# The first half of the retention output projection as seven block products, with block sums made by accumulating DMAs

## The chip, the cores and the metric

The kernel runs on one core of a Trainium2 chip. The metric is the device time of one execution in microseconds; the median of three runs of the kernel before is 2591.95 us. The engines are TensorE (PE, with its weight loads shown as PEld), VectorE (DVE), ScalarE (ACT), GpSimd (POOL) and SyncE (SP), which here only issues DMAs. The weights and activations come from and go to HBM; SBUF holds the tiles and PSUM the sums of TensorE.

## The reference

A trunk of two layers over 1024 tokens and 1024 features, in float32. Layer 0 mixes tokens with forgetting attention, layer 1 with retention, each followed by a SwiGLU FFN. What matters here is the end of retention: `y` is normalized per head, multiplied by a gate, and projected from 2048 features back to 1024.

```python
def retention(h, w_in, w_out):
    ...
    y = y.transpose(1, 0, 3, 2, 4).reshape(B, S, H, dv)
    mu = jnp.mean(y, axis=-1, keepdims=True)
    var = jnp.mean(jnp.square(y - mu), axis=-1, keepdims=True)
    y = ((y - mu) * lax.rsqrt(var + EPS)).reshape(B, S, H * dv).astype(h.dtype)
    return (jax.nn.silu(g) * y) @ w_out
...
            x = x + retention(h, ret_w_in[j], ret_w_out[j])
        h = rmsnorm(x, norm_ffn[i])
        x = x + swiglu(h, ffn_w_in[i], ffn_w_out[i])
```

## The kernel before, in words

All activations are kept transposed: a tile is 128 features by 1024 tokens, used in two halves of 512 tokens (`HALF`). A float32 product is made of three fast ones: each operand is split into a high part (a rounded copy, ScalarE) and a low part (operand minus high part, VectorE) by `split`, lines 98 and 99, and TensorE adds high x high, high x low and low x high (`mm_u`, lines 106 to 108).

Most projections of the kernel do not multiply block by block but by seven products (`Products`, lines 635 to 637): two output tiles by two token halves form a 2 x 2 block, and so do the weights (A11 to A22) and the operand (B11 to B22). The sums S1 to S4 of weight blocks are made by `Blocks`; the sums T1 to T4 of operand blocks by `Combos`, from tiles in SBUF, or by `Stored`, which keeps seven arrays in HBM and loads and splits each when a product first asks for it (`get`, line 560). A product is four triples, 12 matmuls of 512 columns. `open` makes the first product, `middle` the next four, `close` the last two; each pair of output tiles holds three PSUM banks a, b, c from `open` to its last sums. Seven banks go round for these (`mm_ps`).

The retention core has eight stages, four heads by two token halves. `prepare(h)` loads keys, queries and values of a head; `scores`, `weighted` and `crossed` are its matmuls. `finish(h, ib)` takes a stage's four result tiles of 512 tokens, normalizes them (`colsum` and `rows` are small matmuls, lines 159 and 165; the scaling is line 1138), for head 0 multiplies them by the gate that it loads from `gd`, and stores them to `zd` (line 1143). Heads 0 and 1 make z tiles 0 to 7, heads 2 and 3 tiles 8 to 15.

The output projection then runs in two halves over the 16 z tiles. In the first, the eight tiles are loaded by `load_units` (lines 783 and 786), which multiplies head 1's by their gates (line 787) and splits them into 32 buffers of the pool `bpa`; for each of the eight output tiles the weights are loaded and split (`wtile2`, line 773), and `mm_u` makes 8 x 3 matmuls for each half of the tokens; the old residual `xo` is added (lines 1176 and 1177). The second half is `out_proj`, which does the same for tiles 8 to 15 (six of them in the pool `bpb`, of 24 buffers, two in `bpa`), and prepares the next FFN's operand.

What sets the order: the instructions of an engine run in the order of its queue. That order is made at build time by a planner that goes by the written order as priority and by its own estimates of when operands and buffers are free. Buffers limit it: five staging buffers of 1024 columns (`st`), six split buffers for weights (`wh`, `wl`), 16 tiles `y` (`yu`), two buffers `xo`. SP issues nearly all DMAs, from one queue; GpSimd has nothing to do in this part.

Of the kernel before, what the change touches and what calls it, by code (L numbers as in the profile page):

```python
# [17 lines left out]
P = 128  # L18
# [19 lines left out]
def trunk(ctx, tc, nc, d, out):  # L38
# [16 lines left out]
    def nm(s):  # L55
        cnt[0] += 1
        return f"{s}_{cnt[0]}"
# [21 lines left out]
    def wh_wl(width=512):  # L79
        return [wp.tile([P, 512 + 64], F32R, tag=t, name=nm(t))[:, :width] for t in ("wh", "wl")]  # L80
# [20 lines left out]
    def mm_u(ps, wts, acts, h, cols=slice(0, H), first=True, last=True):  # L101
        n = len(wts)
        for k in range(n):
            wh, wl = wts[k]
            xh, xl = (t[:, cols] for t in acts[k][h])
            nc.tensor.matmul(ps, wh, xh, start=(first and k == 0), stop=False)  # L106
            nc.tensor.matmul(ps, wh, xl, start=False, stop=False)  # L107
            nc.tensor.matmul(ps, wl, xh, start=False, stop=(last and k == n - 1))  # L108
# [429 lines left out]
    class Stored:  # L538


        def __init__(self, name, pools):
            self.pools = pools
            self.d = {n: dp.tile([P, 4 * H], F32, tag=name + n, name=name + n) for n in NAMES}
            self.t = {}

        def put(self, j, e, o):
            t1, t2, t4 = qu("t1"), qu("t2"), qu("t4")
            nc.vector.tensor_tensor(t1, e[1], e[0], op=ALU.subtract)
            nc.vector.tensor_tensor(t2, o[1], t1, op=ALU.subtract)
            nc.vector.tensor_tensor(e[1], o[1], e[1], op=ALU.subtract)  # L550
            nc.vector.tensor_tensor(t4, o[0], t2, op=ALU.subtract)
            for n, t in zip(NAMES, (e[0], t2, t1, e[1], o[0], o[1], t4)):
                nc.sync.dma_start(self.d[n][:, j * H:(j + 1) * H], t)

        def get(self, n):
            if n not in self.t:
# [7 lines left out]
    def wsplit(src):  # L564
        hi, lo = wh_wl()
        split(hi, lo, src)
        return hi, lo

    class Blocks:


        def __init__(self, src):
            self.s1, self.ready = None, {}
            sts = []
            for i in range(2):
                st = sp.tile([P, 1024], F32, tag="st", name=nm("st"), bufs=5)
                nc.sync.dma_start(st, src[:, i * 1024:(i + 1) * 1024])
                sts.append(st)
            self.a11, self.a12 = sts[0][:, 0:512], sts[0][:, 512:1024]
            self.a21, self.a22 = sts[1][:, 0:512], sts[1][:, 512:1024]  # L580

        def sums(self, early=False):
            if early:
                self.s1, self.s2 = qu("s1"), qu("s2")
            else:
                self.s1 = sp.tile([P, 512], F32, tag="sc", name=nm("s1"), bufs=4)
                self.s2 = sp.tile([P, 512], F32, tag="sc", name=nm("s2"), bufs=4)
            nc.vector.tensor_tensor(self.s1, self.a21, self.a22, op=ALU.add)  # L588
            nc.vector.tensor_tensor(self.s2, self.s1, self.a11, op=ALU.subtract)

        def early(self):
            self.ready["A11"] = wsplit(self.a11)
# [3 lines left out]
        def get(self, n):  # L596
            if n in self.ready:
                return self.ready[n]
            if n == "A11":
                return wsplit(self.a11)  # L600
            if n == "S2":
                return wsplit(self.s2)
            if n == "S1":
                return wsplit(self.s1)
            if n == "S3":
                nc.vector.tensor_tensor(self.a21, self.a11, self.a21, op=ALU.subtract)
                return wsplit(self.a21)
            if n == "A12":
                return wsplit(self.a12)
# [3 lines left out]
            return wsplit(self.a22)  # L613

    OPERANDS = {"A11": "B11", "S1": "T1", "S2": "T2", "A12": "B21", "S3": "T3", "A22": "T4", "S4": "B22"}

    class Products:
# [26 lines left out]

        def middle(self, u2, u3):

            self.run("S1", self.c, first=True)
            self.run("S2", self.b)
            u2(self.b)
            self.run("A12", self.a)  # L650
            self.run("S3", self.b)
            u3(self.b, self.c)
# [115 lines left out]
    def wtile2(src, nk):  # L768
        parts = []
        for k in range(0, nk, 4):  # L770
            n = min(4, nk - k)
            st = sp.tile([P, 1024], F32, tag="st", name=nm("st"), bufs=5)
            nc.sync.dma_start(st[:, :n * P], src[:, k * P:(k + n) * P])
            hi, lo = wh_wl(n * P)
            split(hi, lo, st[:, :n * P])
            parts += [(hi[:, j * P:(j + 1) * P], lo[:, j * P:(j + 1) * P]) for j in range(n)]
        return parts

    def load_units(pool, src, gate=None):

        r = []
        st = sp.tile([P, 1024], F32, tag="st", name=nm("st"), bufs=5)
        nc.sync.dma_start(st, src)
        if gate is not None:
            gt = sp.tile([P, 1024], F32, tag="st", name=nm("st"), bufs=5)
            nc.sync.dma_start(gt, gate)
            nc.vector.tensor_tensor(st, st, gt, op=ALU.mult)
        for h in range(2):
            r.append(bsplit(pool, st[:, HALF[h]]))
        return r  # L790
# [324 lines left out]
    def finish(h, ib, yps):  # L1115
        acc = sp.tile([P, H], F32, tag="sacc", name=nm("yacc"), bufs=2)
        ys = []
        for vt in range(4):
            y = yu("yt")
            nc.scalar.copy(y, yps[vt])  # L1120
            if vt == 0:
                nc.scalar.activation(acc, y, AF.Square)
            else:
                sq = yu("sq")
                nc.scalar.activation(sq, y, AF.Square)
                nc.vector.tensor_tensor(acc, acc, sq, op=ALU.add)
            ys.append(y)
        cs = colsum(acc, mp, "ms")
        var = small([P, 4], "yv")
        rs = slice(4 * ib, 4 * ib + 4)  # L1130
        nc.vector.scalar_tensor_tensor(var, cs[:, 0:4], 1.0 / 512, rho2[:, h, rs], op0=ALU.mult, op1=ALU.mult)
        nc.vector.tensor_scalar(var, var, EPS, None, op0=ALU.add)
        r = rsqrt(var, 4)
        fac = small([P, 4], "yf")
        nc.vector.tensor_tensor(fac, r, rho[:, h, rs], op=ALU.mult)
        fb = rows(fac, mp, "ms")
        for vt in range(4):
            nc.vector.tensor_tensor(ys[vt], ys[vt], fb, op=ALU.mult)
# [4 lines left out]
            nc.sync.dma_start(zd[4 * h + vt][:, HALF[ib]], ys[vt])  # L1143

    prepare(0)
    heads[0][4] = state(heads[0][1], heads[0][3])
    stages = [(h, ib) for h in range(RET_HEADS) for ib in range(2)]
# [15 lines left out]
        if ib == 1 and nxt:  # L1163
            heads[h + 1][4] = state(heads[h + 1][1], heads[h + 1][3])

    zg = list(zip(zd, [None] * (4 * 1) + gd[4 * 1:]))
# [12 lines left out]
    ffn(1, X, nrm, xd, None, True, nw, MAP3)  # L1179

# [93 lines left out]
```

## Time and profile before

| what | value |
|---|---|
| median of three runs | 2591.95 us (2591.46 to 2592.87) |
| profiled execution | 2590.04 us, of which the span is 2588.2 us |
| TensorE busy | 2561.4 us, 99% of the span |
| VectorE busy | 1839.9 us, 71% |
| ScalarE busy | 1229.7 us, 48% |
| GpSimd busy | 168.0 us, 6% |
| chain of waits, TensorE's share | 94% |

The profile is one execution on the chip. Times in its rows are from the start of the span. A group of instructions is shown with its line, engine, output and inputs, count, busy time and mean duration of one, and then the idle time of the engine just before it and what ended that. Matmuls overlap in their pipeline, so the sum of their durations is more than the time that they take; their cost is read from the distance of their starts. The granted TensorE clock was 0.999 of full speed.

### The profile page before, as it was taken

The numbers are of one execution on the slowest core, as the hardware profiler recorded it, in microseconds if no ns is written. First come the engines' busy times: TensorE is split into PE (matmuls) and PEld (weight loads), VectorE is DVE, ScalarE is ACT, GpSimd is POOL, SyncE is SP. The second block draws the span as 40 slices with busy tenths as digits, with TensorE's granted clock in tenths as the row PEclk, the third lists the DMA queues.
The fourth block names the chain that finished last, engine by engine and source line by source line (L and its number), as shares of the span: only waits on it lengthen the run. The fifth ranks groups of instructions, "written<-read, shape, count | busy, mean of one in ns | idle before, by whom it ended". The sixth has DMA issues, their size and how long they took to land.

```text
span 2588.2 us, 35137 instructions
## 1 busy us (share of the span) xinstructions
PE 2561.4 (99%) x12808; PEld 2182.1 (84%) x12808; DVE 1839.9 (71%) x3131; ACT 1229.7 (48%) x2320; POOL 168.0 (6%) x147
## 2 busy tenths in 40 slices
PE   9999999999999999999999999999999999999998
PEld 8888887888888888889898989898888888888788
DVE  6798888966666768886656576785567666667795
ACT  6566656643333455454343435662354333335543
POOL 0143323000000000001000010000000000000000
PEclk9999999999999999999999999999999999999999
DMA  3111142423332345533332335555522333325441
GB/s 130 45 58 58 58 143 87 160 100 102 110 106 97 120 150 187 165 112 116 101 119 98 110 100 167 191 184 193 202 96 86 106 102 106 105 82 187 167 151 66
DMA packets 137695, 312.12 MB, mean 121 GB/s; under 512 B 15665, under 2 KB 28721, under 8 KB 137521
## 3 DMA queue, kind: packets, MB, share of 16 engines
q1 hardware_dynamic: 136800, 309.33, 35.6%
q8 instruction: 100, 1.64, 0.3%
q14 instruction: 75, 0.61, 0.1%
q10 hardware_dynamic: 720, 0.55, 0.1%
HBM read 217.54 MB, written 92.27 MB: 120 GB/s over the span
## 4 chain that ended last, share of the span: by engine, by line
PE 94%; DVE 2%; issue 1%; ACT 1%; DMA 1%; POOL 0%; SPq 0%; DVEq 0%; POOLq 0%; ACTq 0%
PE mm L635 18%; PE mm L636 18%; PE mm L637 18%; PE mm L107 7%; PE mm L106 7%; PE mm L108 7%; PE mm L751 2%; PE mm L749 2%; PE mm L750 2%; PE mm L256 1%; PE mm L257 1%; PE mm L258 1%; PE mm L1101 1%; PE mm L1102 1%; PE mm L1100 1%
## 5 line engine op out<-in xcount | busy, mean ns | idle before, releaser
L635 PE MATMUL mm<-b,wh 128*128 128x512 f32 x2128 | 826.2, 390 | 3.8 <-ACT 22_4491_22622 L683 2.2
L636 PE MATMUL mm<-b,wh 128*128 128x512 f32 x2128 | 828.3, 389 | 0.0
L637 PE MATMUL mm<-b,wl 128*128 128x512 f32 x2128 | 824.9, 389 | 0.0
L98 ACT CAST wh<-st 128x512 fp32r<-128x512 f32 (+1 forms) x449 | 276.2, 616 | 519.4 <-PE mm L636 315.8
L635 PEld LDWEIGHTS mm<-b,wh 128*128 128x128 f32 x2128 | 399.6, 188 | 86.7 <-ACT 22_4491_22622 L683 2.6
L637 PEld LDWEIGHTS mm<-b,wl 128*128 128x128 f32 x2128 | 399.5, 188 | 82.8
L636 PEld LDWEIGHTS mm<-b,wh 128*128 128x128 f32 x2128 | 399.6, 188 | 82.1
L99 DVE TENSOR_TENSOR wl<-st,wh 128x512 fp32r<-128x512 f32 (+1 forms) x449 | 318.0, 712 | 188.9 <-ACT wh L98 186.1
L98 ACT CAST wh<-s 128x512 fp32r<-128x512 f32 x252 | 156.4, 622 | 307.2 <-PE mm L636 271.5
L106 PE MATMUL mm<-b,wh 128*128 128x512 f32 x736 | 287.0, 393 | 8.4 <-ACT b L126 6.1
L107 PE MATMUL mm<-b,wh 128*128 128x512 f32 x736 | 287.8, 392 | 1.6 <-DVE b L99 1.6
L108 PE MATMUL mm<-b,wl 128*128 128x512 f32 x736 | 287.7, 392 | 0.0
L99 DVE TENSOR_TENSOR wl<-s,wh 128x512 fp32r<-128x512 f32 x252 | 180.0, 716 | 92.9 <-ACT wh L98 88.8
L106 PEld LDWEIGHTS mm<-b,wh 128*128 128x128 f32 x736 | 138.9, 189 | 38.3 <-ACT b L126 6.6
L107 PEld LDWEIGHTS mm<-b,wh 128*128 128x128 f32 x736 | 138.8, 189 | 29.8 <-DVE b L99 2.1
L108 PEld LDWEIGHTS mm<-b,wl 128*128 128x128 f32 x736 | 138.8, 189 | 28.5
L98 ACT CAST b<-st 128x512 fp32r<-128x512 f32 x216 | 124.7, 611 | 79.3 <-DMA st<-ac_T 24.5
L99 DVE TENSOR_TENSOR b<-st,b 128x512 fp32r<-128x512 f32 x216 | 140.7, 675 | 30.3 <-ACT b L98 28.3
L750 PE MATMUL mm<-wl,b 128*128 128x256 f32 x448 | 126.6, 283 | 0.0
L749 PE MATMUL mm<-wh,b 128*128 128x256 f32 x448 | 126.2, 283 | 0.0
L751 PE MATMUL mm<-wh,b 128*128 128x256 f32 x448 | 126.2, 283 | 0.0
L588 DVE TENSOR_TENSOR s<-st 128x512 f32<-128x512 f32 x84 | 58.1, 692 | 66.4 <-DMA st<-ffn_in 27.2
(496 smaller groups left out, 3889.0 us busy)
## 6 DMA issues: line engine op xcount, KB each, us to landing
st<-ffn_in SPq DMA_DIRECT2D x88, 512.0 KB, 3.5
st<-ffn_out_pairs SPq DMA_DIRECT2D x32, 512.0 KB, 3.9
st<-ac_T SPq DMA_DIRECT2D x32, 512.0 KB, 4.9
ac_T<-t SPq DMA_DIRECT2D x48, 256.0 KB, 2.4
st<-ac_B SPq DMA_DIRECT2D x24, 512.0 KB, 4.0
st<-fox_qk SPq DMA_DIRECT2D x32, 256.0 KB, 2.7
xo<-xd SPq DMA_DIRECT2D x32, 256.0 KB, 3.0
ac_B<-t SPq DMA_DIRECT2D x32, 256.0 KB, 2.4
```

Source lines behind the costliest of these rows:

```text
L98: nc.scalar.copy(hi, src)
L99: return nc.vector.tensor_tensor(lo, src, hi.bitcast(F32), op=ALU.subtract)
L106: nc.tensor.matmul(ps, wh, xh, start=(first and k == 0), stop=False)
L107: nc.tensor.matmul(ps, wh, xl, start=False, stop=False)
L108: nc.tensor.matmul(ps, wl, xh, start=False, stop=(last and k == n - 1))
L588: nc.vector.tensor_tensor(self.s1, self.a21, self.a22, op=ALU.add)
L635: nc.tensor.matmul(ps, hi[:, js], th, start=first and j == 0, stop=False, skip_group_check=True)
L636: nc.tensor.matmul(ps, hi[:, js], tl, start=False, stop=False, skip_group_check=True)
L637: nc.tensor.matmul(ps, lo[:, js], th, start=False, stop=(j == 3), skip_group_check=True)
L749: nc.tensor.matmul(o, th[:, tk], hi[:, js], start=f, stop=False, skip_group_check=True)
L750: nc.tensor.matmul(o, th[:, tk], lo[:, js], start=False, stop=False, skip_group_check=True)
L751: nc.tensor.matmul(o, tl[:, tk], hi[:, js], start=False, stop=(j == 3), skip_group_check=True)
```

## The change

The first half of the projection is made by `Products` too. Four pairs of output tiles by seven products replace eight tiles by two halves by eight feature tiles. The even z tiles of heads 0 and 1 are the upper blocks (B11, B12), the odd ones the lower (B21, B22).

`finish` gates heads 0 and 1 itself, B12 and B21 with a minus sign, and stores the four blocks into the arrays of a `Stored` named `zc`. After the second stage of each head, four sums are made in HBM by DMAs that GpSimd issues (`add`): one copies the first summand, the next accumulates the second onto it. With these signs each sum is an addition. `Blocks` gets a form for this weight: its blocks are loaded from two rows of tiles; S2 and A12 are taken with the other sign; and the splits of A11 and A22 (`wsplit_added`) are made by ScalarE (the high part, and its negative into the low part) and two accumulating DMAs, which add the weight from HBM onto the low part. `middle` is cut in two, `before` and `after`, and the order of the 28 products over the four pairs is written out. The z tiles 8 to 15 are gated when they are loaded, as before.

```diff
-        def __init__(self, name, pools):
+        def __init__(self, name, pools, names=()):
...
+        def add(self, js, n, a, b):
+
+            c = slice(js.start * H, js.stop * H)
+            nc.gpsimd.dma_start(self.d[n][:, c], self.d[a][:, c])
+            nc.gpsimd.dma_start(self.d[n][:, c], self.d[b][:, c], accum_op=ALU.add)
...
+    def wsplit_added(src, mem):
+        hi, lo = wh_wl()
+        nc.scalar.copy(hi, src)
+        nc.scalar.activation(lo, src, AF.Copy, scale=-1.0)
+        for q in range(2):
+            nc.gpsimd.dma_start(lo[:, q * 256:(q + 1) * 256].rearrange("p (j c) -> p j c", j=2), mem[:, 2 * q:2 * q + 2],
+                                accum_op=ALU.add)
+        return hi, lo
+
+    def wsplit_neg(src):
+        hi, lo = wh_wl()
+        nc.scalar.activation(hi, src, AF.Copy, scale=-1.0)
+        nc.vector.scalar_tensor_tensor(lo, src, -1.0, hi.bitcast(F32), op0=ALU.mult, op1=ALU.subtract)
+        return hi, lo
...
-                nc.sync.dma_start(st, src[:, i * 1024:(i + 1) * 1024])
+                if self.rows:
+                    for t in range(2):
+                        nc.sync.dma_start(st[:, HALF[t]].rearrange("p (j c) -> p j c", j=4), self.rows[i][:, t])
+                else:
+                    nc.sync.dma_start(st, src[:, i * 1024:(i + 1) * 1024])
...
-            if h < 1:
-                g = yu("g")
-                nc.sync.dma_start(g, gd[4 * h + vt][:, HALF[ib]])
+            if h >= 2:
+                nc.sync.dma_start(zd[4 * h + vt][:, HALF[ib]], ys[vt])
+                continue
+            g = yu("g")
+            nc.sync.dma_start(g, gd[4 * h + vt][:, HALF[ib]])
+            if vt % 2 == ib:
                 nc.vector.tensor_tensor(ys[vt], ys[vt], g, op=ALU.mult)
-            nc.sync.dma_start(zd[4 * h + vt][:, HALF[ib]], ys[vt])
-
+            else:
+                nc.vector.scalar_tensor_tensor(ys[vt], ys[vt], -1.0, g, op0=ALU.mult, op1=ALU.mult)
+            j = 2 * h + vt // 2
+            nc.sync.dma_start(zc.d[(("B11", "B12"), ("B21", "B22"))[vt % 2][ib]][:, j * H:(j + 1) * H], ys[vt])
+        if h < 2 and ib == 1:
+            js = slice(2 * h, 2 * h + 2)
+            zc.add(js, "T1", "B11", "B12")
+            zc.add(js, "T3", "B22", "B12")
+            zc.add(js, "T2", "T1", "B22")
+            zc.add(js, "T4", "T2", "B21")
...
+    zc = Stored("zc", MAP1, ("B12",))
...
-    acts = [load_units(bpa, *t) for t in zg[:8]]
-    for n in range(KT):
-        w = wtile2(d["ret_o"][n], 8)
-        for h in range(2):
-            ps = mm_ps()
-            mm_u(ps, w, acts, h)
-            y[n][h] = yu("y")
-            xo = sp.tile([P, H], F32, tag="xo", name=nm("xo"), bufs=2)
-            nc.sync.dma_start(xo, xd2[n][:, HALF[h]])
-            nc.vector.tensor_tensor(y[n][h], ps, xo, op=ALU.add)
+    def blocks(n):
+        return tuple(d["ret_o"][2 * n + i][:, :D].rearrange("p (j t c) -> p t j c", t=2, c=P) for i in range(2))
...
+    def close(n):
+        p = prods[n]
+        p.close()
+        nc.vector.tensor_tensor(ys[n]["12"], p.c, ys[n]["12"], op=ALU.add)
+        for i in range(2):
+            for h in range(2):
+                u = ys[n][f"{i + 1}{h + 1}"]
+                xo = sp.tile([P, H], F32, tag="xo", name=nm("xo"), bufs=2)
+                nc.sync.dma_start(xo, xd2[2 * n + i][:, HALF[h]])
+                src = (p.a, u)[h] if i == 0 else (p.b, u)[h]
+                nc.vector.tensor_tensor(u, xo, src, op=(ALU.add, ALU.subtract)[i])
+                y[2 * n + i][h] = u
+
+    banks[0] += 1
+    opened(0)
+    before(0)
+    after(0)
+    opened(1)
+    close(0)
+    before(1)
+    after(1)
+    opened(2)
+    close(1)
+    before(2)
+    opened(3)
+    before(3)
+    after(2)
+    close(2)
+    after(3)
+    close(3)
```

`zc` uses MAP1, by which B11, T2 and T1 are split into the 24 buffers of `bpb`, and T3, B21, B22 and T4 into the 32 of `bpa`.

More of the change, by code (lines that the diff above doesn't have):

```diff
@@ L538, in trunk @@
     class Stored:
-        def __init__(self, name, pools):
+        def __init__(self, name, pools, names=()):
             self.pools = pools
-            self.d = {n: dp.tile([P, 4 * H], F32, tag=name + n, name=name + n) for n in NAMES}
+            self.d = {n: dp.tile([P, 4 * H], F32, tag=name + n, name=name + n) for n in NAMES + names}
             self.t = {}
@@ L573, in __init__ @@
             self.s1, self.ready = None, {}
+            self.rows = src if isinstance(src, tuple) else None
             sts = []
@@ L645, in middle, with before @@
         def middle(self, u2, u3):
+            self.before(u2)
+            self.after(u3)
+        def before(self, u2):
             self.run("S1", self.c, first=True)
@@ L649, in middle, with after @@
             u2(self.b)
+        def after(self, u3):
             self.run("A12", self.a)
@@ L1164, in trunk, with opened, before, after @@
             heads[h + 1][4] = state(heads[h + 1][1], heads[h + 1][3])
[L1166 removed]
+    def blocks(n):
+        return tuple(d["ret_o"][2 * n + i][:, :D].rearrange("p (j t c) -> p t j c", t=2, c=P) for i in range(2))
     y = [[None, None] for _ in range(KT)]
[L1168 to L1177 removed]
+    ys = [{} for _ in range(4)]
+    prods = {}
+    def opened(n):
+        prods[n] = Products(blocks(n), zc).open()
+        ys[n].update({q: yu(q) for q in ("11", "12", "21", "22")})
+    def before(n):
+        prods[n].before(lambda b: nc.scalar.copy(ys[n]["12"], b))
+    def after(n):
+        def closed(b, c):
+            nc.scalar.copy(ys[n]["22"], b)
+            nc.vector.tensor_tensor(ys[n]["22"], c, ys[n]["22"], op=ALU.add)
+        prods[n].after(closed)
+    def close(n):
[27 more added lines that the diff above has]
+    close(3)
+    zg = list(zip(zd, gd))
     X, nrm, nw = out_proj(d["ret_o"], y, [load_units(bpb if i < 6 else bpa, *t) for i, t in enumerate(zg[8:])], xd, 3, d["ffn_in"][1, 0], MAP3)
```

13 lines of the change are left out of this document (8 added, 5 removed).

## The prediction

> **What bounds the kernel now.** I read the page first (busy times, the chain of waits, the groups), then what TensorE waited for in the retention layer, then its order of instructions there.
>
> ```profile
> span 2588.2 us, 35137 instructions
> PE 2561.4 (99%) x12808; PEld 2182.1 (84%) x12808; DVE 1839.9 (71%) x3131; ACT 1229.7 (48%) x2320; POOL 168.0 (6%) x147
> ...
> PE 94%; DVE 2%; issue 1%; ACT 1%; DMA 1%; POOL 0%; SPq 0%; DVEq 0%; POOLq 0%; ACTq 0%
> ...
> L635 PE MATMUL mm<-b,wh 128*128 128x512 f32 x2128 | 826.2, 390 | 3.8 <-ACT 22_4491_22622 L683 2.2
> ```
> ```profile
> engine line waited for: us in total, times, longest us
> PE mm L1029 <- DVE wl L1090: 1.1, 1, 1.1
> PE mm L1101 <- DVE wl L1090: 0.3, 1, 0.3
> ```
>
> The second answer is TensorE's waits from 1590 to 1940 us, the whole retention layer behind its projections: 1.4 us in 350. TensorE is the bound here, and a matmul taken out counts in full unless a new wait appears. The seven-product stretches of the FFNs (L635) lost 3.8 us in 2128 triples, so the form by itself runs without holes.
>
> What one matmul costs is its distance to the next, as the 390 ns of a group overlap with the neighbours:
>
> ```profile
> 1752.78 0.40 PE L106 MATMUL mm<-b,wh 128*128 128x512 f32 x1
> ...
> 1765.09 0.39 PE L107 MATMUL mm<-b,wh 128*128 128x512 f32 x1
> ...
> 1771.23 0.39 PE L107 MATMUL mm<-b,wh 128*128 128x512 f32 x1
> ...
> 929.63 0.39 PE L635 MATMUL mm<-b,wh 128*128 128x512 f32 x1
> 936.43 0.39 PE L635 MATMUL mm<-b,wh 128*128 128x512 f32 x1
> ```
>
> Between the two L107 lie nine triples, 27 matmuls in 6.14 us: 0.2274 us each. Between the two L635 lie ten triples: 6.80/30 = 0.2267. One price serves both forms. The first half of the output projection begins at 1752.78; 384 x 0.2274 = 87.3, plus the last two stages' column sums and rows,
>
> ```profile
> 1755.24 0.79 PE cs L159 x8
> ...
> 1763.89 0.89 PE rw L165 x8
> ```
>
> twice each, 3.3 us, puts its end at 1843.4.
>
> **The change part by part.**
>
> *Matmuls.* Removed: 8 tiles x 2 halves x 8 feature tiles x 3 = 384. Added: 4 row pairs x 7 products x 4 x 3 = 336. 48 fewer x 0.2274 = **10.9 us less** on TensorE, all on its path. A product is 12 matmuls, 2.73 us; 28 of them and the 3.3 us end at 1752.8 + 76.4 + 3.3 = 1832.5.
>
> *Gates and stores in the stages.* Head 1 gets eight gate products on VectorE and eight gate loads on SP's queue (256 KB each); four 1024-wide gate products (L787) with their loads of 512 KB and most of the 16 splits of the old operands leave. VectorE works here at
>
> ```profile
> 1700.00:1720.00 20.00, 20.00 (x126) 18.28 (x124) 16.89 (x45) 14.04 (x33) 0.00 (x0) 1.00 0.66 224
> 1720.00:1740.00 20.00, 20.00 (x115) 17.95 (x115) 17.72 (x38) 14.64 (x33) 0.00 (x0) 1.00 0.57 202
> ...
> 1752.78:1843.60 90.82, 90.82 (x418) 75.66 (x417) 51.08 (x86) 22.79 (x42) 0.00 (x0) 1.00 0.65 220
> 1040.00:1058.00 18.00, 18.00 (x81) 14.89 (x81) 18.00 (x31) 10.48 (x20) 0.00 (x0) 1.00 0.58 182
> ```
>
> (columns: length, PE, its weight loads, VectorE, ScalarE, GpSimd, granted clock 1.00, DMA share, GB/s). 16.89 and 17.72 of 20 us. At the prices below, some 13 us leave (4 x 1.15 and 14 x 0.60) and 12 come (8 gates and a dozen of the new splits, x 0.60), so I cost it at nothing. Cover: the spare 2 to 3 us per 20; what exceeds it delays only operands wanted after 1752.
>
> *Block sums.* Four copies and four accumulations per head, 512 KB each, on GpSimd's queue. No row shows a DMA issued there; SP's and ScalarE's rows are the nearest:
>
> ```profile
> zd<-yt SPq DMA_DIRECT2D x32, 256.0 KB, 2.6
> st<-zd SPq DMA_DIRECT2D x16, 512.0 KB, 4.4
> ...
> st<-qd SPq DMA_DIRECT2D x6, 512.0 KB, 6.4
> ```
> ```profile
> q1 hardware_dynamic: 136800, 309.33, 35.6%
> ...
> q10 hardware_dynamic: 720, 0.55, 0.1%
> ```
> ```profile
> 1710.38 2.11 SPq L1143 DMA_DIRECT2D zd<-yt  x4
> ...
> 1790.73 0.32 SPq L783 DMA_DIRECT2D st<-zd  x1
> ```
>
> Bounds for one: 4.4 us below; above, two streams of the slowest loads of this stretch, 12.8, for an accumulation, and 6.4 for a copy. I take 5 and 5, near the lower end, as one 512 KB transfer is nearest to L783's. Head 1's second half is stored at 1710.4; four more gate products (2.4 us), the issue and the landing put it at about 1717. Then T1's sum, the copy to T2, its sum, the copy to T4 follow one another, and GpSimd's queue waits with them: free at 1717 + 20 = 1737, T4 whole at 1742. T1 is wanted at 1755.5 and T4 at 1769 (product 7): hidden. At the upper bounds the queue is free at 1717 + 2 x 12.8 + 2 x 6.4 = 1755.4; behind it stands the first weight split's accumulation (A11 of pair 0, wanted at 1752.8, about 3 us to land), so TensorE would stand 5.6 us there.
>
> By the Trainium skill, page "DMA: Bandwidth & Descriptors", section "Anatomy of one DMA — SWDGE (gpsimd) path", a GpSimd-issued DMA takes about 2.0 us plus its bytes over 436 GB/s; an estimate of 3.2 us for 512 KB, by which the queue would be free at 1730 and the sum stay the same. No run here shows it.
>
> *Weights.* Before, 16 splits; now 28, of which eight (A11, A22) have their low part made by ScalarE and two 128 KB accumulations, off VectorE. Their latency (two ScalarE operations, then 3 to 6 us) lies behind six split buffers, so up to 5 products (13.7 us) early. The loads on SP's queue stay four of 256 KB per pair of tiles, now in runs of 512 bytes for 2 KB:
>
> ```profile
> st<-ret_o SPq DMA_DIRECT2D x26, 256.0 KB, 3.0
> ...
> xo<-xe SPq DMA_DIRECT2D x14, 256.0 KB, 3.0
> ```
>
> 3 us below, twice that above, either inside the same cover. Costed at nothing; without the cover a product would wait some 3 us, eight times.
>
> *VectorE in the first half.* Its own price per 512-wide operation, back to back:
>
> ```profile
> 1040.24 0.68 DVE L720 TENSOR_TENSOR 11_1822_9155<-11_1822_9155,R 128x512 f32<-128x512 f32 x1
> ...
> 1044.46 0.68 DVE L99 TENSOR_TENSOR wl<-st,wh 128x512 fp32r<-128x512 f32 x1
> ...
> 1813.42 1.22 DVE L787 TENSOR_TENSOR st<-st,st 128x1024 f32<-128x1024 f32 x1 [1.69 <-DMA st<-gd]
> ...
> 1831.51 1.23 DVE L787 TENSOR_TENSOR st<-st,st 128x1024 f32<-128x1024 f32 x1 [2.39 <-DMA st<-gd]
> ```
>
> Seven in 4.22 us: 0.60 us, 0.08 under the duration; a gate product of 1024 so takes some 1.15. Each row pair takes 9 operations for its weights and 6 for its results (4 and 4 before): 15 x 0.60 = 9.0 us under 19.1 us of products.
>
> ```profile
> L1138 DVE TENSOR_TENSOR yt<-yt,rw 128x512 f32<-128x512 f32 x8 | 5.0, 682 | 3.0 <-PE rw L165 3.0
> L1126 DVE TENSOR_TENSOR yacc<-yacc,sq 128x512 f32<-128x512 f32 x3 | 2.1, 690 | 0.3 <-ACT sq L1125 0.3
> ```
>
> With these endings of the last two stages (some 9 us with their small operations) and 20 of the 28 operand splits (12 us), 1752 to 1805 holds 2 x 9.0 for pairs 0 and 1, 4.8 for the first sums of 2 and 3: 44 of 52 us.
>
> *The hand-over to the second half* is where I expect the loss. The operands B11, T1, T2 fill all 24 buffers into which six of the last eight z tiles are split; they come free at the ends of products 18, 19, 20: 1805.2, 1808, 1810.7. The next two tiles wait for B21, product 25, 1824.3. From 1805 to 1832.5 VectorE owes 8 x (1.15 + 2 x 0.60) = 18.8 us for these tiles, 22 operations for pairs 2 and 3 less the last 5: 10.2 us, and the first split of the next weights 1.2: 30.2 in 27.3 us. The loads need staging buffers: five, of which the weights of pairs 2 and 3 hold four until about 1808 and two until about 1818. TensorE takes tile k only at 1832.5 + 0.7k, 5 us of slack at the last. From below 0: the FFN's hand-over ran VectorE at 18.00 of 18 us (row 1040 to 1058) with no wait of TensorE, though its six tiles carry no gate. From above: the rate of before, 18.1 us between the gate products at 1813.4 and 1831.5 for five further tiles, 3.6 us each; eight from 1808 + 4.4 end at 1841, and with results pressing in between at 1845, against 1838: 7 us. I take 2.5. Late next: the first group of the second half (L106), then nothing, as the rest of that half is unchanged.
>
> *PSUM and results.* Each pair holds three of seven banks until its last sums, for which two xo buffers are reloaded (256 KB, 3 us): 0 to 3 us in all. The FFN's 3.8 us over 2128/28 = 76 pairs would be 0.2 for four; I take 0.9, as here the first result too stays in its bank until the end.
>
> *Sum.* -10.9 + 2.5 + 0.9 = -7.5 us. The profiled execution took 2590.04 us (span 2588.2 and 1.84 around it), 1.9 below the median of 2591.95; 2582.5 for such an execution, **2584.5 us** for the median. No change is within 0.2%, 5.2 us, about what a measurement of this kernel can tell.
>
> **The rivals.**
>
> *All of it is kept.* For it: the FFN's hand-over; splits can slip into TensorE's 5 us. Against: 30 us of work in 27. 2591.95 - 10.9 = 2581.0.
>
> *The hand-over eats the gain.* One pair of staging buffers until 1818, then 3.6 us per tile as in the rows of L787: 7 us, with PSUM waits up to 8.5. Time 2591.95 - 10.9 + 8.5 = 2589.5. Against it: the order puts eight products behind T2's last use, twice the FFN's cover.
>
> *GpSimd's queue is the new bound* (slower). The sums of head 1 hold the queue, the first A11's low part stands behind them, and TensorE waits at 1752.8. The stall is 2 x (copy + accumulation) + 1717 + 3 - 1752.8; it takes all 7.5 us when copy and accumulation together take 20.2 us, against 10 taken and 19.2 at the bounds. At 23 us for the two the stall is 13.2 and the time 2597.7. For it: nothing in the trace prices this queue, and DMA is already at 0.57 to 0.66 there. Against it: 512 KB moves in 4.4 us.
>
> The added traffic is 8.4 MB for the sums (up to 12.6 if an accumulation counts twice), 2.1 for weights, 3.1 for operands. The stretch of 90.82 us at share 0.65 and 220 GB/s gives 338 GB/s at full share, so 13.6 to 17.8 MB are 40 to 53 us of all engines, over the 165 us from 1665 to 1830: the share rises from 0.6 to between 0.84 and 0.92, which is why the upper bounds are not excluded.
>
> By the Trainium skill, page "DMA: Bandwidth & Descriptors", section "Issuing engines are not separate DMA queues", another issuer brings no other engines, so the sums would slow SP's loads as reckoned here; were it otherwise, this rival would rest on the queue alone. No run so far shows GpSimd's DMAs.
>
> *It does not do what it says* has no case of its own: the count of matmuls falls in any event.
>
> **How the numbers follow.** Forecast with a loss of 1.5 to 5.5 us (2582.5 to 2586.5): 0.45. All kept (2581 to 2582.5): 0.17. Hand-over eats it (2586.8 to 2594): 0.20. GpSimd's queue: 0.18, of which 0.02 end within 0.2%. Faster 0.62, same 0.22, slower 0.16. The range goes from the full gain with 0.5 us of spread, 2580.5, to 2595, which leaves out the worse part of the queue's case. The forecast's own range is 2581 to 2587.
>
> **What would show it.** Right: TensorE has 48 matmuls fewer and no wait over 1 us between 1752 and 1830; one near 1833 behind a split or gate product of 1 to 5 us; VectorE nearly full from 1805 to 1840. Wrong: a wait at the first L635 of the retention layer released by a DMA or by GpSimd; accumulations that land after 10 us or more; waits before products that end at a DMA into the low part; a longer wait at the first L106 of the second half; a loss already in the stages, with VectorE full from 1700 to 1750.

## The result and the profile after

| | before | after |
|---|---|---|
| median (range) | 2591.70 us (2590.87 to 2592.87, 4 runs) | 2618.08 us (2613.97 to 2622.74, 4 runs) |
| profiled execution | 2590.04 us | 2622.74 us (the slowest of its four) |
| granted clock | 0.999 | 0.992 |

The change is slower: ratio 1.0106, 95% interval 1.0093 to 1.0118. The matmuls fell as counted, and the time rose by 26.4 us. The page of the changed kernel (span, busy times, chain of waits, groups):

```profile
span 2621.0 us, 35228 instructions
PE 2566.5 (98%) x12760; PEld 2182.5 (83%) x12760; DVE 1863.7 (71%) x3175; ACT 1251.7 (48%) x2364; POOL 198.2 (8%) x179
...
PE 89%; DMA 3%; DVE 3%; issue 2%; ACT 2%; POOL 0%; SPq 0%; DVEq 0%; POOLq 0%; ACTq 0%
...
L669 PE MATMUL mm<-b,wl 128*128 128x512 f32 x2240 | 872.4, 391 | 12.1 <-DMA wl<-ret_o 12.1
```

12760 matmuls for 12808, but TensorE is *busier*, 2566.5 us for 2561.4, and holds 89% of the chain for 94%. L667 to L669 are the products' three matmuls. What TensorE waited for from 1580 to 1950 us, 1.4 us in the kernel before:

```profile
engine line waited for: us in total, times, longest us
PE mm L669 <- DMA wl<-ret_o: 12.1, 5, 5.2
PE mm L667 <- ACT mm L674: 7.5, 1, 7.5
PE mm L1112 <- ACT yt L1158: 6.0, 1, 6.0
PE mm L1067 <- DVE wl L1128: 2.2, 1, 2.2
```

With three smaller rows, 29.8 us. The first row is the wait for the low parts of A11 and A22, made by accumulating DMAs. The second is the wait for a copy between two PSUM banks (L674). The third stands in the retention core, before any product. The windows (length, TensorE, its weight loads, VectorE, ScalarE, GpSimd, granted clock, DMA share, GB/s) show a second loss:

```profile
1680.00:1700.00 20.00, 20.00 (x119) 18.18 (x118) 14.48 (x39) 10.83 (x26) 3.65 (x5) 1.00 1.02 294
...
1720.00:1740.00 20.00, 13.96 (x71) 12.02 (x70) 13.42 (x36) 10.85 (x26) 1.38 (x2) 0.83 0.76 225
...
1780.00:1800.00 20.00, 17.62 (x67) 13.86 (x68) 16.39 (x32) 14.63 (x29) 3.64 (x3) 0.83 0.83 241
1800.00:1820.00 20.00, 13.94 (x47) 10.83 (x46) 6.79 (x18) 3.13 (x6) 4.84 (x4) 0.74 0.71 175
```

The clock, 1.00 throughout before, falls to 0.74. TensorE's timeline at one wait shows how:

```profile
1772.77 0.39 PE L669 MATMUL mm<-b,wl 128*128 128x512 f32 x1
1780.66 0.80 PE L667 MATMUL mm<-b,wh 128*128 128x512 f32 x1 [7.50 <-ACT mm L674]
1781.25 0.63 PE L668 MATMUL mm<-b,wh 128*128 128x512 f32 x1
1781.68 0.63 PE L669 MATMUL mm<-b,wl 128*128 128x512 f32 x1
...
1786.74 0.39 PE L669 MATMUL mm<-b,wl 128*128 128x512 f32 x1
1786.96 0.39 PE L667 MATMUL mm<-b,wh 128*128 128x512 f32 x1
```

After 7.50 us of idling the matmuls start 0.43 us apart instead of 0.227, until 1786.4: 5.7 us at half speed, so this wait costs about 7.5 + 2.9. By the Trainium skill, page "TensorE: Matmul & The Clock Gate", section "Part 1: The HAM clock gate", an idle window of about 3.4 us halves the clock, and a busy one of about that length restores it. The trace agrees on the half, but not on the lengths: a slow stretch followed the wait of only 2.25 us (L1067) too, and the slow stretches after the waits lasted 3.2 to 8.6 us.

The balance: the first product starts 13.7 us later than the first group of the projection did (1766.5 for 1752.8), the first half takes 109.8 us for 90.8, and the second half starts 32.7 us later. The span of this execution is 32.8 us longer; the medians differ by 26.4.

### The profile page after: what moved, and what is told of

It reads as the page before. It is cut to its first block, busy times and chain, and to the rows that moved or that the text cites. A ratio compares the mean times of both kernels' runs of the same rounds, so it can differ in the third digit from the quotient of the medians.

```text
span 2621.0 us, 35228 instructions
## 1 busy us (share of the span) xinstructions
PE 2566.5 (98%) x12760; PEld 2182.5 (83%) x12760; DVE 1863.7 (71%) x3175; ACT 1251.7 (48%) x2364; POOL 198.2 (8%) x179
## 4 chain that ended last, share of the span: by engine, by line
PE 89%; DMA 3%; DVE 3%; issue 2%; ACT 2%; POOL 0%; SPq 0%; DVEq 0%; POOLq 0%; ACTq 0%
PE mm L667 19%; PE mm L668 19%; PE mm L669 19%; PE mm L106 6%; PE mm L107 6%; PE mm L108 6%; PE mm L789 2%; PE mm L787 2%; PE mm L788 2%; DMA st<-vd 1%; PE mm L256 1%; PE mm L257 1%; PE mm L258 1%; DMA wl<-ret_o 1%; PE rw L165 1%
## 5 line engine op out<-in xcount | busy, mean ns | idle before, releaser
L667 PE MATMUL mm<-b,wh 128*128 128x512 f32 x2240 | 874.7, 391 | 10.7 <-ACT mm L674 7.5
L669 PE MATMUL mm<-b,wl 128*128 128x512 f32 x2240 | 872.4, 391 | 12.1 <-DMA wl<-ret_o 12.1
L669 PEld LDWEIGHTS mm<-b,wl 128*128 128x128 f32 x2240 | 422.6, 189 | 101.9 <-DMA wl<-ret_o 12.3
L667 PEld LDWEIGHTS mm<-b,wh 128*128 128x128 f32 x2240 | 422.5, 189 | 99.3 <-ACT mm L674 7.9
L98 ACT CAST wh<-st 128x512 fp32r<-128x512 f32 (+3 forms) x437 | 268.8, 616 | 479.5 <-PE mm L668 319.0
L99 DVE TENSOR_TENSOR wl<-st,wh 128x512 fp32r<-128x512 f32 (+3 forms) x437 | 309.7, 711 | 178.1 <-ACT wh L98 175.8
L98 ACT CAST wh<-s 128x512 fp32r<-128x512 f32 x264 | 164.0, 622 | 313.6 <-PE mm L668 280.1
L99 DVE TENSOR_TENSOR wl<-s,wh 128x512 fp32r<-128x512 f32 x264 | 188.0, 714 | 96.9 <-ACT wh L98 92.6
L98 ACT CAST b<-st 128x512 fp32r<-128x512 f32 x228 | 132.8, 612 | 103.8 <-DMA st<-ac_T 25.2
L99 DVE TENSOR_TENSOR b<-st,b 128x512 fp32r<-128x512 f32 x228 | 149.7, 676 | 43.9 <-ACT b L98 40.7
```

What stands on the lines that cost most here:

```text
L98: nc.scalar.copy(hi, src)
L99: return nc.vector.tensor_tensor(lo, src, hi.bitcast(F32), op=ALU.subtract)
L667: nc.tensor.matmul(ps, hi[:, js], th, start=first and j == 0, stop=False, skip_group_check=True)
L669: nc.tensor.matmul(ps, lo[:, js], th, start=False, stop=(j == 3), skip_group_check=True)
```

## The experiments

Two theories to begin with: the loss is the low parts made through GpSimd, or it is the block sums' DMAs. For the sums, three ways to cost: T1 to T4 come late, their traffic slows other transfers, or an in-order engine's work stands behind a load that they delay. The kernel before ran beside each group of kernels, with medians of 2590.64, 2590.07, 2590.79, 2590.74 and 2590.81 us in the order of the groups. Where an expectation has a letter for a theory, the words beside it say which it is. The planner orders every kernel anew, so an edit can also move instructions that it does not name.

**Low parts and sums, each alone.**

```diff
# e1: A11 and A22 split by VectorE (as every other block)
-                return wsplit_added(self.a11, self.rows[0][:, 0]) if self.rows else wsplit(self.a11)
+                return wsplit(self.a11)
# e2: no sums; T1, T2 are read from B11, T3 from B22, T4 from B21
-            zc.add(js, "T1", "B11", "B12")   # and the other three
# e3: both
```

> A11 and A22 are split by ScalarE and VectorE as every other weight; no accumulation into a low part is left, the block sums stay. Theory A (two sorts of accumulating DMAs, each with its own share of the loss): TensorE's waits for the low part (12.1 us in the profile after) and the half-speed stretches behind them go, some 15 to 18 us: 2600 to 2605 us. Theory B (the low parts are only where a general lateness of that half shows, made by staging buffers and VectorE): VectorE gets eight operations more, the waits move to other releasers, 2613 to 2620 us. Theory C (the low parts are all of the loss): 2584 to 2590 us.

> The sixteen DMAs of the block sums are left out (leaves out work: T1 and T2 are read from B11, T3 from B22, T4 from B21, as many loads as before); the accumulations into low parts stay. Theory A: the waits in the retention stages (6.0, 2.2 us and the late start of the products) and the 7.5 us wait of the first pair go, with their half-speed stretches: 2598 to 2606 us, the core stages again ending near 1753 us. Theory B: the stages are late by the moved gates, not by DMA traffic, and stay late: 2612 to 2620. Theory C: little changes, 2612 to 2620.

> Both edits together (leaves out work, as the run without block sums does): the seven products, their order, the moved gates and loads, without any DMA issued by GpSimd. Theory A: what the matmul count and the hand-over give, 2582 to 2587 us, TensorE's waits in the layer under 5 us. Theory B: 2600 us or more, with waits at the hand-over and in the first pair.

Measured: e1 2598.81 us (ratio 1.0031, 1.0021 to 1.0042), e2 2601.20 (1.0038, 1.0023 to 1.0053), e3 2587.94 (0.9986, 0.9977 to 0.9996). So the low parts cost 13.3 us without sums (e2 - e3) and 19.3 with them (changed kernel - e1); the sums cost 10.9 without low parts (e1 - e3) and 16.9 with them (changed kernel - e2). Both have a share, and together they cost some 6 us more than one by one. e1 lies 1.2 below and e3 0.9 above the range of its theory A.

**How the sums cost.** In e5 they run and nobody reads them; e10 makes the accumulations plain copies of the same bytes.

```diff
# e5 = e1, and get() reads T1, T2 from B11, T3 from B22, T4 from B21
# e10 = e5, and in add():
-            nc.gpsimd.dma_start(self.d[n][:, c], self.d[b][:, c], accum_op=ALU.add)
+            nc.gpsimd.dma_start(self.d[n][:, c], self.d[b][:, c])
```

> The splits by VectorE; the sixteen DMAs of the block sums run, but nothing reads what they write (leaves out work: T1 and T2 are read from B11, T3 from B22, T4 from B21, as in the run with neither, 2587.9 us). Theory A1 (the sums cost by their traffic: the loads of v, the stores and the gates land later while DMA is full, VectorE and ScalarE wait, TensorE waits and then runs at half speed): as slow as with the sums read, 2597 to 2601 us, the core stages ending near 1766 us. Theory A2 (they cost because T1 to T4 are ready late): as fast as with neither, 2586 to 2590 us, the stages ending near 1756.

> As the kernel whose sums run unread (2600.6), but the eight accumulating DMAs in memory are plain copies of the same bytes from the same queue. Still not the full computation: the products read the unsummed blocks. If the cost of the sums is bytes on the DMA engines, whatever is done with them: 2597 to 2601. If it is the accumulating (a read, an add and a write of the destination): halfway or more towards the kernel without sums, 2588 to 2594.

e5: 2600.56 (1.0040, 1.0027 to 1.0053), as dear as e1, so it isn't that T1 to T4 come late. e10: 2596.08 (1.0017, 1.0006 to 1.0028), between its two ranges and a third of the way from e5 to e3. So about two thirds of the cost stay with plain copies of the same bytes, and about a third goes with the accumulating: the eight DMAs of line 559 landed after a median of 8.8 us as accumulations (e5) and of 5.2 as copies (e10). The DMA view of the changed kernel from 1600 to 1900 us (issuing queue, count, KB each, median us from issue to landing; POOLq is GpSimd's):

```profile
st<-ret_o SPq DMA_DIRECT2D x29, 256.0 KB, 4.3
st<-vd SPq DMA_DIRECT2D x24, 256.0 KB, 4.4
zcT<-zcB POOLq DMA_DIRECT2D x12, 512.0 KB, 8.1
...
zcT<-zcT POOLq DMA_DIRECT2D x4, 512.0 KB, 6.3
wl<-ret_o POOLq DMA_DIRECT2D x16, 128.0 KB, 5.1
```

512 KB within memory take 6.3 us as a copy (zcT<-zcT) and 8.1 in the row that mixes four copies with eight accumulations; the accumulations alone (line 559) have a median of 8.1 too. By the Trainium skill, page "DMA: Bandwidth & Descriptors", section "Anatomy of one DMA — SWDGE (gpsimd) path", the prediction estimated 3.2 us. The runs show about twice that and more. By the Trainium skill, page "DMA: Bandwidth & Descriptors", section "Issuing engines are not separate DMA queues", the DMAs of all issuers run on the same 16 engines. The runs agree: beside the unread sums of e5, SP's loads st<-vd landed after a median of 4.5 us, in e3 after 3.5.

**The sums without memory.** VectorE adds them (e4, e6), or GpSimd's adders (e9), from first-stage tiles that are kept; e6 and e9 hold the gates in the `xo` buffers. The block sums of e6, which also puts T2 into a buffer of another pool, do not come out as the others' do, so it is read for its queues alone.

```diff
# e4 (e9: nc.gpsimd for nc.vector, T1 to T4 stored from GpSimd's queue)
+                nc.vector.tensor_tensor(b11, b11, b12, op=ALU.add)
+                nc.sync.dma_start(zc.d["T1"][:, c], b11)
...
# e6, e8, e9, e13, e14
-            g = yu("g")
+            g = sp.tile([P, H], F32, tag="xo", name=nm("g"), bufs=2)
```

> The whole computation without GpSimd: the splits by VectorE, and the block sums by VectorE in the second stage of a head, from the first stage's four tiles that are kept in SBUF (eight additions of 512 columns per head, some 4.8 us; six stores more per head, no copies). Theory A: 2583 to 2590 us, a little over the run with neither, as VectorE is at 0.85 in these stages. Theory B: 2600 or more.

> As the run with sums and splits by VectorE (2597.7 us, the stages ending at 1770.9, the first half in 81.6 us), but the gate tile of a stage comes from the two xo buffers, idle there, and T2 from an idle buffer of another pool, so that five fewer of the sixteen y tiles are wanted at once. If those stages were late because ScalarE's copies out of PSUM waited for a y tile: the stages end near 1755, 2582 to 2587 us. If VectorE's eight additions and the gates are the cause: 2594 to 2599 us, unchanged.

> The run with neither (sums left out, 2587.9 us) with the gate tiles in the xo buffers. If the y tiles are what makes the stages end 3.0 us later than before (1755.8 for 1752.8): 1753 and 2583 to 2586 us. If it is the work of head 1's gates on VectorE and SP: no change, 2587 to 2589 us.

> Full computation, with neither an accumulation nor a copy in memory. A11 and A22 are split by VectorE; the sixteen block sums are made by GpSimd's own adders (512 columns take 1.45 us there in the profile of before) from the first stages' tiles, which are kept, and their results are stored from GpSimd's queue, so that no load of the products stands behind them on SP's queue; the gate tiles go into the xo buffers. If the extra cost of the sums is the DMA engines' share (the traffic falls from 24 reads and writes between memories to 8 stores): 2585 to 2590, the time of the kernels without sums (2584.9 and 2587.9). If it is the y tiles held until the sums are made (as where VectorE made them, 2597.7): 2594 to 2600, with ScalarE's copies out of PSUM waiting for a y tile.

e4 2597.69 (1.0029, 1.0017 to 1.0041), e6 2602.75 (1.0048, 1.0033 to 1.0063) and e9 2614.35 us (1.0088, 1.0073 to 1.0103): e4 lies between its two ranges, e6 and e9 above theirs. What e9's TensorE waited for:

```profile
PE cs L159 <- DVE yacc L1164: 21.8, 2, 13.7
```

The column sums at a stage's end wait for the squares, and these, in ScalarE's waits, 15.4 us for stores out of `y` tiles to land, as the tiles kept for the sums leave few free. In e4 the same row of TensorE has 8.2 us. With tiles freed, e6's stages end at 1752.4 as before, but TensorE waits 10.5 us at the second half's first group: SP issues its weights only at 1850.6, behind the loads of the z tiles. e8 (no sums, gates in `xo`) is 2584.85 (0.9976, 0.9967 to 0.9986), 3.1 below e3. In the two profiled executions, though, the first product starts later (1757.5 for 1755.8) and the second half ends at the same time (1928.7 and 1928.8), so the 3.1 us are not shown to come from these stages. No version of the sums without memory is faster than the kernel before.

**The low parts' transfers.** With the weights laid out in the order in which a block is read, a low part is one accumulation of 2 KB runs instead of two of 512 bytes.

```diff
# e7 (no sums), e11 (with sums)
-        for q in range(2):
-            nc.gpsimd.dma_start(lo[:, q * 256:(q + 1) * 256].rearrange("p (j c) -> p j c", j=2), mem[:, 2 * q:2 * q + 2],
-                                accum_op=ALU.add)
+        nc.gpsimd.dma_start(lo, mem, accum_op=ALU.add)
```

> No block sums (left out as before, 2601.2 us with the accumulations as they are); the weights lie in memory so that each low part is one accumulation of 2 KB runs (128 rows of 256 KB) in place of two of 512-byte runs, one behind the other. Theory S (the price is that of the small runs and of the second DMA that waits for the first): the low part lands 4 to 6 us behind its copy, TensorE's 11.2 us of waits shrink below 3, 2588 to 2592 us. Theory P (the price is the accumulation as such, or its place in the planner's order): 2597 to 2602 us.

> The changed kernel, full computation, with one edit: the weights of this projection lie in memory in the order in which a block is read, so that a low part is one accumulation of 2 KB runs in place of two of 512-byte runs. Without sums this edit took 7.9 us away (2601.2 to 2593.3). If the two costs only add: 2608 to 2611. If the low parts stand above all behind the sums' DMAs on GpSimd's queue and the DMA engines, with few waits for the low parts themselves: 2614 or more. If most of the 30 us is one tangle of both, with half clock after each wait: 2600 to 2606.

e7 2593.34 (1.0008, 0.9999 to 1.0018), 7.9 below e2 and 1.3 above the range of its theory S; e11 2607.23 (1.0064, 1.0049 to 1.0079), 10.9 below the changed kernel and between two of its ranges. TensorE's waits for low parts, in e2 and then in e7:

```profile
PE mm L669 <- DMA wl<-ret_o: 11.2, 5, 3.7
```
```profile
PE mm L667 <- DMA wl<-ret_o: 2.0, 1, 2.0
```

So more than half of the low parts' price without sums goes when one DMA with long runs replaces two in turn with short ones; what is left in e7 against e3 is 5.4 us. Whether the number of DMAs or the length of the runs matters is not separated, and the new layout also lengthens the runs of SP's weight loads.

**The order behind the delayed loads.** ScalarE's timeline in the changed kernel ahead of the waits at L1112 (6.0 us) and at the first product's copy L674 (7.5 us):

```profile
1719.88 1.33 ACT L1048 ACTIVATE b<-st,vmean 128x512 fp32r<-128x512 f32 x2
1729.25 0.62 ACT L98 CAST b<-st 128x512 fp32r<-128x512 f32 x1 [8.04 <-DMA st<-zcB]
1729.78 1.06 ACT L1158 COPY yt<-mm 128x512 f32<-128x512 f32 x2
...
1774.42 1.14 ACT L98 CAST b<-st 128x512 fp32r<-128x512 f32 x2 [9.29 <-DMA st<-zcB]
...
1780.01 0.59 ACT L674 COPY mm<-mm 128x512 f32<-128x512 f32 x1
```

The cast of B11, not wanted before 1752, stands ahead of the copies out of PSUM (L1158) for which TensorE waits, and its load is late. The copy L674 stands in the same way behind a cast that waited 9.29 us, and behind the ten operations after it: from the cast's start to the copy it is 5.6 us. The rows of ScalarE's waits, 1640 to 1780 us, in e1, then in e3, say how late the sums make the loads:

```profile
ACT b L1048 <- DMA st<-vd: 26.2, 8, 5.0
ACT b L98 <- DMA st<-zcB: 17.2, 3, 6.1
```
```profile
ACT b L98 <- DMA st<-zcB: 13.8, 6, 5.6
ACT b L1048 <- DMA st<-vd: 12.5, 8, 3.6
```

e12 holds back casts on ScalarE and names nothing else; e13 adds the gates in `xo`, e14 also issues the loads of T1 to T4 from GpSimd.

```diff
# e12 = e1, and (copied: ScalarE's copies L1158 in written order)
+    with tc.issue_after(copied[4 * 6 + 3]):
+        opened(0)
+        before(0)
```

> Full computation: as the kernel with A11 and A22 split by VectorE (2598.8), and one more edit, an order alone: ScalarE's casts for the first four products are queued behind its copies out of PSUM of the seventh stage, so that no copy stands behind a load that is late. If the sums cost through that order: the 5.8 us wait of TensorE for a y tile at about 1722 and the 5 us of half clock behind it go, the stages end near 1757 in place of 1767.8, and the time is 2588 to 2592. If the sums cost through the DMA engines' share wherever the casts stand: 2596 to 2600, with the wait at another place.

> Full computation: as the one before, with the gate tiles in the xo buffers in place of y tiles, which without sums took 3.1 us away. If ScalarE's order was the sums' price: 2585 to 2589, below the kernel before. If the share of the DMA engines is: 2594 to 2598.

> Full computation: as the one before, and the loads of T1 to T4 are issued from GpSimd's queue, behind the sums, so that SP's queue, held for 20.1 us by loads of sums not yet made, goes on. If SP's held queue still costs (loads of weights and of the second half behind it): 2 to 4 us below the one before. If not: within 2 us of it, or above, as two 512 KB loads are then issued by GpSimd for each sum.

e12 2593.41 (1.0011, 1.0001 to 1.0020): 5.4 below e1, 1.4 above the range of its first case, and the wait of 5.8 us is 0.5. The work is the same, so the gain is order; but it is not ScalarE's order alone, as the planner also moved SP's DMAs. Four stores of z tiles, issued from 1743.8 in e1 behind two loads of sums, are issued from 1732.9 in e12, ahead of them. What is left stands at the second half's first group:

```profile
PE mm L106 <- ACT wh L98: 3.2, 1, 3.2
...
PE mm L1112 <- ACT yt L1158: 0.5, 1, 0.5
```

e13 2600.98 (1.0039, 1.0026 to 1.0052) lies outside both of its ranges: the `xo` gates, beside a gain of 3.1 us in e8, come with a loss of 7.6 here and with 6.2 us of new waits of TensorE for VectorE's `wl` (L1128) in the retention core. Why was not settled. e14 2603.32 (1.0044, 1.0030 to 1.0057) is 2.3 above e13: SP's held queue shows no price of its own.

**Both orders repaired.** The second half's first weights are loaded before its last two (e15) or last four (e16) z tiles; e17 does as e15 with the low parts by accumulations; e18 as e15 without sums.

```diff
# e16 = e12, and (e15: 6 for 4); out_proj uses `first` as its first weights
+    acts = [load_units(bpb, *t) for t in zg[8:12]]
+    first = wtile2(d["ret_o"][0, :, D:], 8)
+    acts += [load_units(bpb if i < 6 else bpa, *t) for i, t in enumerate(zg[8:]) if i >= 4]
```

> Full computation: as the kernel with ScalarE's casts behind the copies (2593.4), and the first weights of the second half are loaded and split before the last two of its eight z tiles. If the hand-over's wait is the order of those loads: its 3.2 us and about 4 us of half clock go, 2586 to 2589, below the kernel before. If the last z tiles, pushed back by two loads, are waited for in their place: 2590 to 2595.

> Full computation: the same with the first weights of the second half before the last four z tiles. If the order is enough with two tiles, this is 0 to 3 us above it, since its split buffers and staging buffers are taken earlier.

> The changed kernel, full computation, with its accumulations into the low parts of A11 and A22, and the two orders of the first of these runs (casts behind the copies, the second half's first weights before its last two z tiles). If order is the whole loss: within 4 us of that run. If the low parts keep a price of their own, 13.3 us without sums and 19.3 with them: 13 to 19 us above it, 2600 to 2608.

> Sums left out (T1 and T2 are read from B11, T3 from B22, T4 from B21), A11 and A22 split by VectorE, and the two orders. If the sums cost through order alone, within 2 us of the first of these runs. If their traffic keeps a price: 4 to 10 us below it, 2580 to 2584, near the 2581.0 at which the whole gain is kept.

e15 2589.24 us (0.9993, 0.9984 to 1.0002), e16 **2586.47** (0.9988, 0.9979 to 0.9997), e18 2587.68 (0.9989, 0.9980 to 0.9998), e17 2619.12 (1.0106, 1.0092 to 1.0120). e16 came 2.8 below e15, where 0 to 3 above had been expected, and e17 29.9 above e15, outside both of its ranges. With the orders repaired, leaving the sums out gains nothing that can be measured (e18 is 1.6 below e15 and 1.2 above e16); and without sums the two orders gain nothing (e18 is 0.3 below e3). e16's two longest waits, and then one window of e16 and of e18:

```profile
PE mm L667 <- ACT mm L674: 3.0, 1, 3.0
PE mm L1067 <- DVE wl L1128: 2.2, 1, 2.2
```
```profile
1720.00:1740.00 20.00, 20.00 (x124) 18.30 (x123) 14.96 (x45) 11.22 (x30) 2.75 (x4) 1.00 0.83 254
```
```profile
1720.00:1740.00 20.00, 20.00 (x117) 17.98 (x116) 13.43 (x44) 9.72 (x27) 0.00 (x0) 1.00 0.28 108
```

The DMA share is 0.83 with the sums and 0.28 without, and TensorE is full in both; in the changed kernel it worked 13.96 us of these 20 at a share of 0.76. The traffic cost through the order. e16 makes the whole computation and is a little faster than the kernel before; in its profile the last matmul of the second half starts at 1926.6, before at 1930.4.

e17 and e15 differ by edit in the low parts alone: 29.9 us. GpSimd's timeline in e17, and TensorE's row that follows:

```profile
1758.65 0.82 POOL L559 DMA_DIRECT2D zcT<-zcB  x1 [8.12 <-DMA zcT<-zcT]
1759.39 1.35 POOL L582 DMA_DIRECT2D wl<-ret_o  x1
1768.30 1.22 POOL L582 DMA_DIRECT2D wl<-ret_o  x1 [7.56 <-issue]
```
```profile
1768.01 0.80 PE L669 MATMUL mm<-b,wl 128*128 128x512 f32 x1 [11.69 <-DMA wl<-ret_o]
```

The first low part stands behind the last sum of head 1 on GpSimd's queue: this is the prediction's slower rival, with 11.7 us where it had reckoned 5.6 at its bounds and 13.2 at 23 us for the two DMAs. TensorE stops at 1756.3, GpSimd issues the low part 3.1 us later, and it lands 8.6 us after that, so most of this wait is the landing. In the changed kernel both halves of the first low part were issued ahead of that last sum, and no wait for them shows before the first product, which was itself 13.7 us late.

## Why the prediction was wrong

It gave 2584.5 us, 2580.5 to 2595.0; 2618.08 came.

- *Matmuls*: right. 48 fewer, and e16, with both costs taken away, is 4.3 us under the kernel before, where 7.5 was forecast. TensorE's waits in the layer are 5.9 us in e16 and 1.4 in the kernel before.
- *Weights, the step that failed most.* "3 to 6 us behind six split buffers, so up to 5 products early, costed at nothing." The two accumulations of one low part follow one another: the second is issued 3.6 to 7.0 us after the first in the changed kernel, 8.9 in the rows of e17. And the cover isn't there. The row of ScalarE's waits, 1755 to 1870 us, in the changed kernel:

```profile
ACT wh L579 <- PE mm L668: 17.3, 5, 8.9
```

  ScalarE can begin a split (L579) only when TensorE gives a buffer back, and waits up to 8.9 us for that; the DMAs begin after it. The prediction named the price without the cover, "some 3 us, eight times", which is 24 us and of the size measured (13.3, 19.3 and 29.9 in the three pairs), but put nothing into the sum and left it out of the range.
- *Block sums.* Priced at 5 and 5 us, bounds 4.4 and 6.4 to 12.8; measured 6.3 for copies and 8.1 for accumulations (medians), inside the bounds. "Hidden" was right as to the operands T1 to T4 (e5) and wrong as to the other loads. The prediction reckoned the DMA share at 0.84 to 0.92 from 1665 to 1830 (measured 0.80) and drew no cost from it. The step left out: which instruction stands behind a late load on an in-order engine. It was 10.9 us without the low parts, and two changes of order took it away.
- *GpSimd's queue*, chance 0.18: in e17 its mechanism stands at the first product, but the terms were mis-sized. The first accumulation for head 1 is issued at 1729.9, not about 1717, and the low part lands after 8.6 us, not about 3. With the terms as measured (issued at 1759.4) its sum gives 15.2 us from 1752.8, and 11.7 from 1756.3, where TensorE was by then. In the changed kernel no wait at the first product is of this kind: there the first accumulation for head 1 is issued at 1734.4, since the stores came late, and the low part went ahead of the last sum.
- *Gates and stores in the stages*: "nothing" is near. Without sums the stages end at 1755.8 in e3 and the first product starts at 1752.7 in e18, against 1752.8.
- *Hand-over*, 2.5 us: the mechanism was another one. In the changed kernel no wait shows there. Where one does, the last z tiles were not waited for; the first weights behind them were, 3.2 us in e12.
- *PSUM and results*, 0.9 us: too small. TensorE waited 7.5 us for the copy L674 in the changed kernel, since ScalarE stood behind a late load, and still 2.2 in e15 and 3.0 in e16.
- *Half clock behind waits* stood in no term. Stages and first half exceed the floor (1752.8, and 90.8 - 10.9) by 13.7 + 29.9 = 43.6 us. The waits explain 28.4 (29.8 less the 1.4 of before). For most of the other 15.2 the half clock stands: behind five waits TensorE worked for 26.3 us in all at a granted clock of 0.50, which costs 13.1.

Of the prediction's signs of being wrong, the waits that end at a DMA into the low part came (12.1 us), and so did a loss already in the stages, but without VectorE full: it worked 13.42 us of the 20 from 1720 to 1740.

## What to carry to other kernels

A DMA in place of an engine's operation is not free, even where that engine was the busy one: price it by its landing under the traffic of that stage, add the ones queued ahead of it, and ask when its input buffer is released, as a pool of buffers covers only what the release lets start. When traffic grows, look on each in-order engine for work that is wanted now behind a load that is wanted later; moving that work was worth as much here as removing the traffic (e15 and e16 against e18). A wait of TensorE of several microseconds should be priced with the half-speed stretch behind it.

## What the runs showed of the hardware

- After idling for 7.50 us TensorE ran at half pace, 0.43 us a matmul, for 5.7 us. How long an idle time must be for that did not come out as one number: in the changed kernel a slow stretch followed 2.25 us of idling and none followed 1.44, while in e5 one of 3.5 us followed 1.38 us, with another short wait just before, and in the kernel before none followed 2.2 us at 2427.
- A DMA within memory of 512 KB issued by GpSimd landed after 6.3 us (copy) under this load. The same eight DMAs landed after a median of 8.8 us as accumulations (e5) and of 5.2 as copies (e10).
- Two 128 KB accumulations in 512-byte runs into one tile were issued 3.6 to 8.9 us apart in the changed kernel and e17; for five of the eight pairs of the changed kernel the view shows no releaser but "issue". One of 256 KB in 2 KB runs landed after a median of 7.5 us in e7 and 6.7 in e11.
- The DMA share of a window is shown above 1 (1.02 at 294 GB/s) with TensorE full in that window, so a high share did not by itself stop TensorE.
